# GpSimd's arithmetic in two token mixers handed to VectorE, and modulation rows with places of their own

## The chip, the cores and the metric

The kernel runs on one core of a Trainium2 chip. The core has five engines, each with its own instruction queue, worked in order: TensorE (PE; its weight loads are listed as PEld), VectorE (DVE), ScalarE (ACT), GpSimd (POOL) and SyncE (SP), which issues nearly all DMAs here. Data lie in SBUF (128 partitions) or, behind a matmul, in PSUM banks of 512 columns. The metric is the device time of one execution in microseconds (us).

## The reference, cut to what matters

A backbone of two layers works on 256 latent tokens and 256 context tokens of width 1024. Everything is fp32.

```
for li in range(2):
    sh1, sc1, g1, sh2, sc2, g2 = split(silu(c) @ w_mod[li] + b_mod[li], 6)     # and the same for c_ctx
    h = rms_norm(x) * (1 + sc1) + sh1
    zp, zr, zq, zk, zv, zg = split(h @ w_in[li], ...)
    branches = pool(zp), rwkv7(zr, both directions), attention(zq, zk, zv)     # three mixers
    y = sum_n(sigmoid(zg[n]) * (branches[n] @ w_branch[li, n])) @ w_out[li]
    x = x + g1 * y
    h = rms_norm(x) * (1 + sc2) + sh2
    x = x + g2 * (swiglu(h) if li == 0 else top-2 of 8 experts(h))
```

Context tokens run through layer 0 in full; in layer 1 they only feed the RWKV state and the attention.

## The kernel before

Every large matmul has fp32 accuracy from three passes: a weight tile (128 x 1024, L220, DMA on SP) is split into a rounded part `whi` (ACT, L204) and the rest `wlo` (L208, on DVE or POOL), and whi times x-high, whi times x-low and wlo times x-high are summed in PSUM (L246 to L248, or as a generator L491 to L493). Raw weights, `whi` and `wlo` have two places each in the pool `wa`. In the mixers and in the dense feed-forward every second `wlo` is made by POOL (`lo_mod` 2, `lo_pool` 1), in the experts none.

A mixer has these stages. The front makes the RWKV operands, channel group by channel group and direction by direction (`operands`, L643 to L651), and the pooling; L523 to L527 take each projection out of PSUM with its shift. Then attention, and beside it a triangular solve on DVE (`solve`). Then the core: eight chunks for two directions, each with grams (L871), masks of them on DVE (L882 Ga, L877 Gr), reads (Y, L931), the solved XV (L942 on DVE, L943 on ACT) and the state (XV sum L960, state S L962 on POOL). A chunk of the kept operands comes by DMA (`rakbv`, L845), and its part `Ga` again in a second place (L861), where POOL multiplies it by the decay (L862). Between the core's steps PE is given fill: gate projections and branch merges of the generator `dense`, interleaved by fixed ratios, so PE's order is written out. Readout, merge with the RWKV branch and the output projection follow.

`dense` also advances `mod_slow`: modulation vectors as row products on DVE. A tile of 128 rows of `w_mod2` (128 x 1024) comes by DMA into the next raw weight place (L364), DVE multiplies it by the condition and sums (L368 twice, half a row each, for the context; L370, a whole row in place, for the latents). Layer 0's core does 24 such tiles for layer 0; the dense feed-forward does 56 more.

The scheduler fills DVE, ACT, POOL and SP in the order that its own estimate of times gives; where PE's order is manual it follows the code. Layer 1's second half begins with routing (norm, logits, rank, mask, selection, L1693 to L1794), while the first experts' weights are loaded and split ahead.

```
e = nc.gpsimd if lo_eng == "pool" else nc.vector
e.tensor_tensor(lo, src, hi.bitcast(F32), op=OP.subtract)          # L207, L208
w = self.raw()                                                     # L363, mod_slow
nc.sync.dma_start(a, src[p, :, 64:128])                            # L861, chunk
nc.gpsimd.tensor_tensor(a, a, g[q].to_broadcast([64, 4, 64]), op=OP.mult)
```

Of the kernel before, what the change touches and what calls it, by code (L numbers as in the profile page):

```python
# [19 lines left out]
D = 1024  # L20
# [83 lines left out]
class Builder:  # L104
    def __init__(self, ctx, tc, I, out, dbg=None):
        self.ctx, self.tc, self.nc, self.I, self.out = ctx, tc, tc.nc, I, out
        self.dbg = dbg or {}
        self.nlo, self.lo_first = 0, 0
        self.pre, self.ahead = [], []
        self.raws, self.parted, self.pin = (), (), False  # L110
        self.nraw = self.nparts = 0
        self.banks = {}
        self.norm_banks = ExitStack()
        self.sq = self.rs = None
        self.hw = 512
        self.cpool = ctx.enter_context(tc.tile_pool(name="consts", bufs=1))
        self.dram = ctx.enter_context(tc.tile_pool(name="dr", bufs=1, space=DRAM))
        nc = self.nc
        cst = self.cpool.tile([128, C_N], F32, name="cst")
        nc.sync.dma_start(cst, I["cst"])  # L120
        self.cst = cst
        self.ident = cst[:, C_ID:C_ID + 128]
        self.mask = cst[:, C_MSK:C_MSK + 128]
        self.i2 = cst[:, C_I2:C_I2 + 64]
        self.ob = cst[:, C_OB:C_OB + 128]
        self.ones = cst[:, C_ON:C_ON + 128]
        self.tiny = ctx.enter_context(tc.tile_pool(name="tiny", bufs=6))
        hb = self.cpool.tile([40, 4, 128], F32R, name="hb")
        with tc.tile_pool(name="hb0", bufs=1) as hp:
            hb0 = hp.tile([40, 4, 128], F32, name="hb0")  # L130
            nc.sync.dma_start(hb0, I["heads"])
            nc.vector.tensor_copy(hb, hb0)
        self.hb = hb
        self.vec = []
        for l in range(2):
            v = self.cpool.tile([128, V_N], F32, name=f"vec{l}")
            nc.sync.dma_start(v, I["vec"][l])
            self.vec.append(v)
        self.mod = [[None] * 6 for _ in range(2)]
# [61 lines left out]
    def split(self, hi, lo, src, hi_eng="act", lo_eng="dve"):  # L201
        nc = self.nc
        if hi_eng == "act":
            nc.scalar.copy(hi, src)  # L204
        else:
            nc.vector.tensor_copy(hi, src)
        e = nc.gpsimd if lo_eng == "pool" else nc.vector  # L207
        e.tensor_tensor(lo, src, hi.bitcast(F32), op=OP.subtract)  # L208

    def wload(self, src, n, lo_eng=None, hi_eng="act"):  # L210
# [20 lines left out]
        for s, raw in raws:  # L231
            self.split(hi[:, s], lo[:, s], raw[:, :s.stop - s.start], hi_eng, lo_eng)
        return hi, lo
# [119 lines left out]

    def mod_slow(self, l, j):

        nc = self.nc
        m = self.cpool.tile([128, KD, 2], F32, name=f"mod{l}_{j}")
        b = self.vec[l][:, V_BMOD + 8 * j:V_BMOD + 8 * j + 8]
        ni = 2 if l == 0 or j < 2 else 1
        st = self.mp.tile([128, KD, 2], F32, name="mst", tag="mst")  # L360
        s2 = self.mp.tile([128, KD, 2], F32, name="mst2", tag="mst2")
        for f in range(KD):
            w = self.raw()  # L363
            nc.sync.dma_start(w, self.I["w_mod2"][l, j, f])  # L364
            if ni == 2:
                for h, a in enumerate((st, s2)):
                    k = slice(512 * h, 512 * h + 512)
                    nc.vector.scalar_tensor_tensor(self.scr(), w[:, k], 0.5, self.cb[:, 1, k], op0=OP.mult,  # L368
                                                   op1=OP.mult, accum_out=a[:, f, 1:2])
            nc.vector.scalar_tensor_tensor(w, w, 0.5, self.cb[:, 0], op0=OP.mult, op1=OP.mult,  # L370
                                           accum_out=st[:, f, 0:1])
            yield 3.0
        if ni == 2:
            nc.vector.tensor_tensor(st[:, :, 1], st[:, :, 1], s2[:, :, 1], op=OP.add)
        nc.vector.tensor_tensor(m[:, :, :ni], st[:, :, :ni], b.unsqueeze(2).to_broadcast([128, KD, ni]), op=OP.add)
        self.mod_done(l, j, m[:, :, :ni])
# [174 lines left out]
    def rwkv_front(self, l, full, order):  # L551
# [19 lines left out]
        nc.sync.dma_start(lw, I["lora"][l])  # L571
        self.split(lwh, lwl, lw, "act", "pool")
        self.g2 = sv.tile([96, 512], F32, name="g2")
# [26 lines left out]
        def glo_tile():  # L600
            glo = yield from self.shifted_out(l, 1, T_GLO, full, self.u)
            nc.scalar.activation(glo[0:96, :], glo[0:96, :], AF.Tanh, scale=0.5)
            nc.gpsimd.tensor_scalar(glo[0:96, :], glo[0:96, :], 0.5, 0.5, op0=OP.mult, op1=OP.add)
            self.glo = glo
# [17 lines left out]
        def operands(c, d):  # L622
# [24 lines left out]
                                    n4(G)[:, :, :, :63], o4(kk)[:, :, :, 1:], op=OP.mult)  # L647
            nc.gpsimd.tensor_copy(st[:, :, 1, 0].rearrange("p (s n) -> p s n", s=2), o4(kk)[:, :, :, 0])
            nc.scalar.copy(s4(4), o4(vc))
            nc.gpsimd.tensor_tensor(s4(0), n4(G), o4(rc), op=OP.mult)  # L650
            nc.gpsimd.tensor_tensor(self.order(kd, 0), self.order(kd, 0), self.order(rc, d), op=OP.mult)  # L651
            return st, kd
# [93 lines left out]
    def out_gates(self, l, n, order):  # L746
# [4 lines left out]
        for c in range(4):  # L751
# [5 lines left out]
            gate = self.og.tile([128, n], F32, name="og", tag="og")  # L757
            nc.scalar.copy(gate, gp)
            nc.gpsimd.tensor_scalar(bo, bo, v[:, V_GNB + c:V_GNB + c + 1], None, op0=OP.add)
            nc.gpsimd.tensor_tensor(bo, bo, gate, op=OP.mult)  # L760
            nc.sync.dma_start(self.bonus[c], bo)
            nc.gpsimd.tensor_scalar(gate, gate, v[:, V_GNG + c:V_GNG + c + 1], None, op0=OP.mult)
            nc.sync.dma_start(self.gain[c], gate)
# [75 lines left out]
    def chunk(self, d, n, need_o):  # L839
# [17 lines left out]
        if n:  # L857
            g = self.gq[d][:, :, n - 1].unsqueeze(2)
            for hh, p, q in self.HEADS:
                a = e["Ga"][q, hh]  # L860
                nc.sync.dma_start(a, src[p, :, 64:128])  # L861
                nc.gpsimd.tensor_tensor(a, a, g[q].to_broadcast([64, 4, 64]), op=OP.mult)  # L862
        return e
# [81 lines left out]
    def state(self, e, new, d, n):  # L945
# [15 lines left out]
        for hh, p, q in self.HEADS:  # L961
            nc.gpsimd.tensor_tensor(nS[q], new["XV"][q, hh], g[q].to_broadcast([64, 4, 64]), op=OP.mult)  # L962
        return nS
# [71 lines left out]
    def readout(self, l, n, pool):  # L1035
# [13 lines left out]
        for c in range(4):  # L1049
# [3 lines left out]
            nc.scalar.activation(sq, w, AF.Square)  # L1053
            nc.gpsimd.tensor_tensor(ga[c], ga[c], w, op=OP.mult)
            sqs.append(sq)
# [126 lines left out]
    def pool_branch(self, l, full, order):  # L1182
# [6 lines left out]
        def pool_tile(g):  # L1189
# [10 lines left out]
            for i, z in enumerate(zs):  # L1200
# [3 lines left out]
                while w < win:  # L1204
                    nxt = self.pb.tile([128, 272], F32, name="z", tag="z")
                    nc.gpsimd.tensor_tensor(nxt[:, :m - w], cur[:, :m - w], cur[:, w:m], op=OP.add)
                    cur, m, w = nxt, m - w, 2 * w
                ti = t[:, 256 * i:256 * i + 256]
                nc.gpsimd.tensor_tensor(ti, cur[:, 8 - h:264 - h], iv, op=OP.mult)
                nc.gpsimd.tensor_tensor(ti, ti, z[:, 8:264], op=OP.subtract)  # L1210
            order.add(2, mixed(g, t), self.waits[5] * ns * (g + 4))
# [10 lines left out]

    def branch_split(self, tiles, n, mixed=False):
        res = []
        for t in tiles:
            hi = self.u2(n, F32R)
            lo = self.u2(n, F32R)
            self.split(hi, lo, t, "act", "dve" if mixed and len(res) % 2 == 0 else "pool")
            res.append((hi, lo))
        return res  # L1230

    def merge_branch(self, l, b, br, f, full, gate, acc):
# [8 lines left out]
        if acc is None:  # L1241
            return gate
        nc.gpsimd.tensor_tensor(acc, acc, gate, op=OP.add)
        return acc
# [9 lines left out]
    def merge_steps(self, l, b, br, f, full, gate, acc):  # L1254
# [9 lines left out]
        if acc is not None:  # L1264
            nc.gpsimd.tensor_tensor(acc, acc, gate, op=OP.add)

    def mixer(self, l, x, full, xnew, done=lambda: None):
# [12 lines left out]
        self.sp_small = ex.enter_context(P("small", 1))  # L1280
        self.lo_mod, self.lo_pool, self.lo_first = 2, 1, 2
        self.raws, self.parted = (self.wa, self.wa) + tuple(ex.enter_context(P("w", 1)) for _ in range(l)), (self.wa,)
# [115 lines left out]
        def early_gate(f):  # L1398
            g = lambda n: self.gp.tile([128, n], F32, name="gp", tag="gp")
            self.gate[f] = yield from self.gate_steps(l, 1, f, full, g, "pool")  # L1400

        def dense():
            mods = (t for i in self.parts[4 + l] for t in self.mod_slow(*i))
            br = self.branch_split(self.nat, n)
# [69 lines left out]
        for c in range(4):  # L1474
            self.dump(f"rw{c}", self.wkv[c])
            self.dump(f"nat{c}", self.nat[c])
            self.dump(f"pool{c}", self.pool[c])
        br = self.branch_split(self.wkv, n, True)
        m = []
# [38 lines left out]
    def ffn(self, l, x):  # L1518
        nc, tc, I = self.nc, self.tc, self.I
        with ExitStack() as ex:  # L1520
# [33 lines left out]
            with tc.manual_schedule(engines={mybir.EngineType.PE}):  # L1554
                for f in range(2):
# [10 lines left out]
                    early(f, raws, pss)  # L1566
            mods = (t for i in self.parts[10] for t in self.mod_slow(*i))
            for f in range(2, KF):
# [86 lines left out]
    def moe(self, l, x):  # L1655
        nc, tc, I = self.nc, self.tc, self.I
        ident = self.ident
        with ExitStack() as ex:
# [21 lines left out]
            with P2("scrm2", 3) as self.sp, tc.high_priority(100000):  # L1680
# [40 lines left out]
                keep(nc.vector.tensor_copy(pos, pp.rearrange("p (t e) -> p t e", e=8)))  # L1721
                sel = self.selected(0, pos, msk, two, keep)
                for t in range(2):
# [403 lines left out]
```

## Time and profile before

| | us |
|---|---|
| median of 3 runs | 2495.73 |
| lowest, highest | 2491.53, 2501.99 |
| the profiled execution | 2494.59 |
| its span, first to last instruction | 2492.8 |

Over the span PE is busy 93%, DVE 73%, ACT 51%, POOL 23%, and the DMA queues move 514 MB at a mean of 206 GB/s. By time the stages are, roughly: layer 0's front to 205 us, attention to 410, the core to 655, readout, merge and projection to 780, the dense feed-forward to 1130, layer 1's front to 1300, attention to 1490, the core to 1615, readout and routing to 1690, the experts to the end. Shares over the whole span mix these stages; a stage is read from its own stretch.

[...] A row of waits names who waited and what released it; "issue" means that the profile shows no releaser.

### The profile page before, as it was taken

The numbers are of one execution on the slowest core, as the hardware profiler recorded it, in microseconds if no ns is written. First come the engines' busy times: TensorE is split into PE (matmuls) and PEld (weight loads), VectorE is DVE, ScalarE is ACT, GpSimd is POOL, SyncE is SP. The second block draws the span as 40 slices with busy tenths as digits, with TensorE's granted clock in tenths as the row PEclk, the third lists the DMA queues.
The fourth block names the chain that finished last, engine by engine and source line by source line (L and its number), as shares of the span: only waits on it lengthen the run. The fifth ranks groups of instructions, "written<-read, shape, count | busy, mean of one in ns | idle before, by whom it ended". The sixth has DMA issues, their size and how long they took to land. (4 is left out here: it accounts for less than half of the span.)

```text
span 2492.8 us, 40223 instructions
## 1 busy us (share of the span) xinstructions
PE 2318.3 (93%) x15206; PEld 1858.1 (75%) x15206; DVE 1809.5 (73%) x2723; ACT 1276.6 (51%) x1864; POOL 576.6 (23%) x487
## 2 busy tenths in 40 slices
PE   6899999988899999999779889979999999999998
PEld 4567667777678888777566678768888888888876
DVE  3784667656677656875785755568999999989997
ACT  3553554222243222234554444347777777777775
POOL 1255421243351221122553335430000000000000
PEclk8999998999899999999989989989999999999999
DMA  6364233554433444772473326675999999999995
GB/s 250 95 168 132 77 98 93 173 151 154 144 118 104 150 144 144 235 241 78 128 186 97 116 89 198 194 262 177 367 351 339 360 363 336 343 361 344 356 343 194
DMA packets 224141, 514.33 MB, mean 206 GB/s; under 512 B 70490, under 2 KB 104666, under 8 KB 222786
## 3 DMA queue, kind: packets, MB, share of 16 engines
q1 hardware_dynamic: 223938, 511.67, 61.1%
q8 instruction: 122, 2.00, 0.3%
q14 instruction: 81, 0.66, 0.1%
HBM read 484.79 MB, written 26.74 MB: 205 GB/s over the span
## 5 line engine op out<-in xcount | busy, mean ns | idle before, releaser
L204 ACT CAST whi<-wraw 128x1024 fp32r<-128x1024 f32 (+2 forms) x753 | 754.3, 1019 | 615.9 <-DMA wraw<-in_ffn 178.9
L208 DVE TENSOR_TENSOR wlo<-wraw,whi 128x1024 fp32r<-128x1024 f32 (+2 forms) x629 | 756.4, 1232 | 137.3 <-ACT whi L204 126.5
L208 POOL TENSOR_TENSOR wlo<-wraw,whi 128x1024 fp32r<-128x1024 f32 (+2 forms) x124 | 263.9, 2129 | 722.3 <-ACT whi L204 714.6
L491 PE MATMUL mm<-h,whi 128*128 128x512 f32 (+1 forms) x864 | 347.7, 402 | 33.3 <-DVE s L527 13.6
L493 PE MATMUL mm<-h,wlo 128*128 128x512 f32 (+1 forms) x864 | 321.4, 372 | 11.9 <-DVE wlo L208 6.2
L492 PE MATMUL mm<-h,whi 128*128 128x512 f32 (+1 forms) x864 | 322.0, 373 | 5.5 <-DVE h L476 5.4
L1845 PE MATMUL mm<-whi,xh 128*128 128x512 f32 (+1 forms) x768 | 289.2, 377 | 0.0
L1846 PE MATMUL mm<-whi,xl 128*128 128x512 f32 (+1 forms) x768 | 288.1, 375 | 0.0
L1847 PE MATMUL mm<-wlo,xh 128*128 128x512 f32 (+1 forms) x768 | 281.5, 376 | 1.3 <-DVE wlo L208 1.3
L491 PEld LDWEIGHTS mm<-h,whi 128*128 128x128 f32 x864 | 172.4, 200 | 86.2 <-issue 36.1
L493 PEld LDWEIGHTS mm<-h,wlo 128*128 128x128 f32 x864 | 172.2, 199 | 42.7 <-DVE wlo L208 8.5
L492 PEld LDWEIGHTS mm<-h,whi 128*128 128x128 f32 x864 | 172.9, 200 | 33.5 <-DVE h L476 9.2
L247 PE MATMUL mm<-h,whi 128*128 128x512 f32 (+1 forms) x448 | 170.6, 382 | 2.6 <-DVE h L208 2.6
L248 PE MATMUL mm<-h,wlo 128*128 128x512 f32 (+1 forms) x448 | 170.8, 382 | 0.4 <-POOL wlo L208 0.3
L246 PE MATMUL mm<-h,whi 128*128 128x512 f32 (+1 forms) x448 | 169.8, 380 | 0.0
L1847 PEld LDWEIGHTS mm<-wlo,xh 128*128 128x128 f32 x768 | 144.1, 188 | 29.2 <-DVE wlo L208 2.1
L1846 PEld LDWEIGHTS mm<-whi,xl 128*128 128x128 f32 x768 | 144.4, 188 | 27.0
L1845 PEld LDWEIGHTS mm<-whi,xh 128*128 128x128 f32 x768 | 144.6, 188 | 26.5
L1874 PE MATMUL mm<-wlo,hh 128*128 128x512 f32 x352 | 139.6, 397 | 0.8 <-DVE wlo L208 0.8
L1873 PE MATMUL mm<-whi,hl 128*128 128x512 f32 x352 | 139.1, 395 | 0.0
L1872 PE MATMUL mm<-whi,hh 128*128 128x512 f32 x352 | 138.7, 394 | 0.0
L368 DVE SCALAR_TENSOR_TENSOR scr<-wraw,cb 128x512 f32<-128x512 f32 x96 | 75.7, 806 | 57.6 <-DMA wraw<-in_w_mod 57.0
(378 smaller groups left out, 4024.4 us busy)
## 6 DMA issues: line engine op xcount, KB each, us to landing
wraw<-in_moe SPq DMA_DIRECT2D x516, 512.0 KB, 5.5
wraw<-in_w_in SPq DMA_DIRECT2D x108, 512.0 KB, 3.7
wraw<-in_w_mod SPq DMA_DIRECT2D x96, 512.0 KB, 4.6
wraw<-in_ffn SPq DMA_DIRECT2D x60, 512.0 KB, 3.9
rakbv<-std SPq DMA_DIRECT2D x32, 640.0 KB, 5.3
wraw<-in_w_branch SPq DMA_DIRECT2D x48, 256.0 KB, 2.7
std<-st SPq DMA_DIRECT2D x16, 640.0 KB, 5.0
wraw<-in_w_out SPq DMA_DIRECT2D x13, 512.0 KB, 4.1
```

The costliest lines, as they stand in the source:

```text
L204: nc.scalar.copy(hi, src)
L208: e.tensor_tensor(lo, src, hi.bitcast(F32), op=OP.subtract)
L246: nc.tensor.matmul(ps, wh, xh, start=i == 0, stop=False)
L247: nc.tensor.matmul(ps, wh, xl, start=False, stop=False)
L248: nc.tensor.matmul(ps, wl, xh, start=False, stop=i == n - 1)
L491: nc.tensor.matmul(ps, wh, xh, start=i == 0, stop=False)
L492: nc.tensor.matmul(ps, wh, xl, start=False, stop=False)
L493: nc.tensor.matmul(ps, wl, xh, start=False, stop=i == n - 1)
L1845: nc.tensor.matmul(ps, xh[:, k0 + k], hi[:, w], start=k0 + k == 0, stop=False)
L1846: nc.tensor.matmul(ps, xl[:, k0 + k], hi[:, w], start=False, stop=False)
L1847: nc.tensor.matmul(ps, xh[:, k0 + k], lo[:, w], start=False, stop=k0 + k == 7)
L1874: nc.tensor.matmul(y, hid[k][0], lo[:, w], start=False, stop=k == KF - 1)
```

## The change

In the mixers POOL keeps only its memsets. The weight splits, the splits of activations, the pooling sums, `Ga` and `S` of the core, two operand products, the branch sums and the readout product go to DVE; one small copy, a tanh rescaling and the gate's gain go to ACT; the gate path loses its PSUM copy. The dense feed-forward keeps POOL's splits (`lo_mod` 2 there as before). Layer 0's `mod_slow` no longer takes raw weight places but two half-row tiles from the pool `u` (13 places in layer 0), and its latent product is done in two halves (L374 twice, L377 twice). In the experts the third and the fourth weight split of DVE are ordered behind the last instruction of the selection.

```
-        self.split(lwh, lwl, lw, "act", "pool")
+        self.split(lwh, lwl, lw, "act", "dve")
-            nc.gpsimd.tensor_copy(st[:, :, 1, 0].rearrange("p (s n) -> p s n", s=2), o4(kk)[:, :, :, 0])
+            nc.scalar.copy(st[:, :, 1, 0].rearrange("p (s n) -> p s n", s=2), o4(kk)[:, :, :, 0])
-            nc.gpsimd.tensor_tensor(s4(0), n4(G), o4(rc), op=OP.mult)
-            nc.gpsimd.tensor_tensor(self.order(kd, 0), self.order(kd, 0), self.order(rc, d), op=OP.mult)
+            nc.vector.tensor_tensor(s4(0), n4(G), o4(rc), op=OP.mult)
+            nc.vector.tensor_tensor(self.order(kd, 0), self.order(kd, 0), self.order(rc, d), op=OP.mult)
...
-            nc.scalar.copy(gate, gp)
-            nc.gpsimd.tensor_scalar(bo, bo, v[:, V_GNB + c:V_GNB + c + 1], None, op0=OP.add)
-            nc.gpsimd.tensor_tensor(bo, bo, gate, op=OP.mult)
+            nc.vector.scalar_tensor_tensor(bo, bo, v[:, V_GNB + c:V_GNB + c + 1], gp, op0=OP.add, op1=OP.mult)
...
-                nc.gpsimd.tensor_tensor(a, a, g[q].to_broadcast([64, 4, 64]), op=OP.mult)
+                nc.vector.tensor_tensor(a, a, g[q].to_broadcast([64, 4, 64]), op=OP.mult)
-            nc.gpsimd.tensor_tensor(nS[q], new["XV"][q, hh], g[q].to_broadcast([64, 4, 64]), op=OP.mult)
+            nc.vector.tensor_tensor(nS[q], new["XV"][q, hh], g[q].to_broadcast([64, 4, 64]), op=OP.mult)
...
-        self.lo_mod, self.lo_pool, self.lo_first = 2, 1, 2
+        self.lo_mod, self.lo_pool, self.lo_first = 2, 0, 0
...
-            w = self.raw()
-            nc.sync.dma_start(w, self.I["w_mod2"][l, j, f])
+            ws = place()
+            for s, w in ws:
+                nc.sync.dma_start(w, self.I["w_mod2"][l, j, f][:, s])
...
-            nc.vector.scalar_tensor_tensor(w, w, 0.5, self.cb[:, 0], op0=OP.mult, op1=OP.mult,
-                                           accum_out=st[:, f, 0:1])
+            for (s, w), a in zip(ws, (st, s2)):
+                nc.vector.scalar_tensor_tensor(w, w, 0.5, self.cb[:, 0, s], op0=OP.mult, op1=OP.mult,
+                                               accum_out=a[:, f, 0:1])
...
-            mods = (t for i in self.parts[4 + l] for t in self.mod_slow(*i))
+            mods = (t for i in self.parts[4 + l] for t in self.mod_slow(*i, lambda: [(slice(512 * h, 512 * h + 512), self.u()) for h in range(2)]))
...
+            ins = self.split(hi[:, s], lo[:, s], raw[:, :s.stop - s.start], hi_eng, lo_eng)
+            if self.nlo in self.late_lo:
+                self.behind(ins)
...
-                sel = self.selected(0, pos, msk, two, keep)
+                sel = self.selected(0, pos, msk, two, lambda ins: setattr(self, "mark", keep(ins)))
+
+                self.late_lo = (3, 4)
```

DVE's queue in layer 0's core, one step of the chunks, before: Y copies, a modulation row, the masks.

```order
L931 COPY Y_5056<-ch_5047 128x256
L931 COPY Y_5067<-ch_5058 128x256
L368 SCALAR_TENSOR_TENSOR scr_5390,mst_4882<-wraw_5388,cb_126 128x512
L368 SCALAR_TENSOR_TENSOR scr_5392,mst2_4883<-wraw_5388,cb_126 128x512
L370 SCALAR_TENSOR_TENSOR wraw_5388,mst_4882<-wraw_5388,cb_126 128x1024
L882 TENSOR_TENSOR Ga_5023<-sm_5078,cst_60 64x256
L877 TENSOR_TENSOR Gr_5026<-sm_5078,cst_60 128x256
```

The same engine in a step of layer 0's core now; `u` tiles are modulation rows, L868 is the Ga product that POOL did (L862 before).

```order
L868 TENSOR_TENSOR Ga_4458<-Ga_4458,gq0_3970 64x256 x2
L374 SCALAR_TENSOR_TENSOR scr_4515,mst2_4027<-u_4510,cb_126 128x512
L868 TENSOR_TENSOR Ga_4471<-Ga_4471,gq1_3971 64x256
L377 SCALAR_TENSOR_TENSOR u_4509,mst_4026<-u_4509,cb_126 128x512
L868 TENSOR_TENSOR Ga_4471<-Ga_4471,gq1_3971 64x256
L1271 TENSOR_TENSOR u2_2467<-u2_2467,u_4337 128x512
L888 TENSOR_TENSOR Ga_4458<-sm_4533,cst_60 64x256
L883 TENSOR_TENSOR Gr_4461<-sm_4533,cst_60 128x256
```

The row products still stand ahead of the masks, in more and smaller pieces, and the Ga products, each behind its own DMA, have come in between.

SP's queue in the same core, before: weights and modulation rows take turns in the two raw places.

```order
L845 DMA rakbv_5034<-std01_84 128x4x320
L856 DMA r_5040<-std01_84 64x4x64 x2
L220 DMA wraw_5240<-in_w_in 128x1024
L364 DMA wraw_5388<-in_w_mod2 128x1024
L861 DMA Ga_5023<-std00_83 64x4x64 x2
L861 DMA Ga_5036<-std01_84 64x4x64 x2
L220 DMA wraw_5396<-in_w_in 128x1024
```

SP's queue there now, with half rows into `u`.

```order
L862 DMA r_4758<-std01_84 64x4x64 x2
L867 DMA Ga_4741<-std00_83 64x4x64 x2
L867 DMA Ga_4754<-std01_84 64x4x64 x2
L369 DMA u_4791<-in_w_mod2 128x512
L369 DMA u_4792<-in_w_mod2 128x512
L369 DMA u_4901<-in_w_mod2 128x512
L369 DMA u_4902<-in_w_mod2 128x512
L221 DMA wraw_5193<-in_w_branch 128x512
```

Rows are now asked for two at a time, and no weight load stands behind a row in the same place.

DVE's queue in layer 1's core, where there are no modulation rows, before.

```order
L931 COPY Y_14286<-ch_14277 128x256
L931 COPY Y_14297<-ch_14288 128x256
L1263 SCALAR_TENSOR_TENSOR u_14132<-u_14132,mm_14244 128x256
L882 TENSOR_TENSOR Ga_14253<-sm_14305,cst_60 64x256
L877 TENSOR_TENSOR Gr_14256<-sm_14305,cst_60 128x256
```

And now.

```order
L937 COPY Y_14345<-ch_14336 128x256
L937 COPY Y_14356<-ch_14347 128x256
L1269 SCALAR_TENSOR_TENSOR u_14191<-u_14191,mm_14303 128x256
L868 TENSOR_TENSOR Ga_14312<-Ga_14312,gq0_13412 64x256
L1271 TENSOR_TENSOR u2_12383<-u2_12383,u_14191 128x256
L868 TENSOR_TENSOR Ga_14312<-Ga_14312,gq0_13412 64x256
L209 TENSOR_TENSOR wlo_14515<-wraw_14512,whi_14514 128x1024
L888 TENSOR_TENSOR Ga_14312<-sm_14364,cst_60 64x256
L883 TENSOR_TENSOR Gr_14315<-sm_14364,cst_60 128x256
```

Two Ga products, a branch sum and a weight split, all POOL's or spread over both before, now stand between Y and the masks.

## Rows read from the trace of the kernel before

**Rows 1.** Busy time by stage: stretch, length, engines (instructions), clock, DMA share, GB/s.
```profile
110.00:205.00 95.00, 83.91 (x518) 60.33 (x518) 79.37 (x79) 53.38 (x90) 61.34 (x54) 0.93 0.67 166
...
430.00:655.00 225.00, 201.88 (x2230) 160.18 (x2229) 137.04 (x288) 52.76 (x101) 75.53 (x73) 0.93 0.50 153
...
780.00:1130.00 350.00, 344.47 (x1487) 277.42 (x1486) 236.38 (x349) 100.31 (x138) 75.35 (x33) 1.00 0.55 178
...
1200.00:1300.00 100.00, 80.11 (x624) 63.38 (x623) 82.86 (x91) 60.22 (x104) 57.80 (x51) 0.91 0.66 170
...
1490.00:1615.00 125.00, 119.99 (x1956) 107.18 (x1955) 65.38 (x141) 49.00 (x103) 63.60 (x79) 1.00 0.62 184
...
1690.00:2493.00 803.00, 790.24 (x3829) 655.81 (x3827) 722.96 (x745) 604.48 (x677) 1.82 (x1) 1.00 0.90 327
```

**Rows 2.** PE's waits, 430 to 660: releaser, us in total, times, longest.
```profile
PE sm L871 <- issue: 9.4, 2, 4.8
PE ch L917 <- ACT XV L943: 7.8, 4, 3.9
PE ch L928 <- DVE Ga L882: 3.9, 2, 3.4
PE ch L939 <- DVE Y L931: 1.1, 1, 1.1
PE sm L871 <- DVE Gr L877: 0.7, 3, 0.3
```

**Rows 3.** DVE's groups, 430 to 655: busy us, mean ns, idle before and releaser.
```profile
L368 DVE SCALAR_TENSOR_TENSOR scr<-wraw,cb 128x512 f32<-128x512 f32 x40 | 34.2, 856 | 45.9 <-DMA wraw<-in_w_mod 45.6
...
L882 DVE TENSOR_TENSOR Ga<-sm,cst 64x256 f32<-64x256 f32 x32 | 13.5, 420 | 8.0 <-PE sm L871 7.3
```

**Rows 4.** DVE in order of time, 526 to 546: start, duration, idle before.
```profile
534.87 0.69 DVE L368 SCALAR_TENSOR_TENSOR scr<-wraw,cb 128x512 f32<-128x512 f32 x1 [6.14 <-DMA wraw<-in_w_mod]
...
538.08 0.41 DVE L882 TENSOR_TENSOR Ga<-sm,cst 64x256 f32<-64x256 f32 x1
```

**Rows 5.** PE in order of time, the same stretch.
```profile
538.92 0.76 PE L871 MATMUL sm<-rakbv 64*128 64x128 f32 x2 [4.61 <-issue]
```

**Rows 6.** Waits of the DMA queue SP, 430 to 660.
```profile
SPq L220 <- DVE wraw L370: 42.1, 7, 9.9
SPq L220 <- DVE wlo L208: 19.0, 5, 4.7
```

**Rows 7.** DVE's groups, 1710 to 2490, where POOL is idle.
```profile
L208 DVE TENSOR_TENSOR wlo<-wraw,whi 128x1024 fp32r<-128x1024 f32 x505 | 598.8, 1222 | 46.3 <-ACT whi L204 36.5 <-PE mm L1847 2.9 <-PE sm L1855 2.2
L1860 DVE TENSOR_TENSOR hl<-sm,hh 128x512 fp32r<-128x512 f32 x40 | 27.4, 684 | 0.0
```

**Rows 8.** POOL's groups over the whole span.
```profile
L208 POOL TENSOR_TENSOR wlo<-wraw,whi 128x1024 fp32r<-128x1024 f32 x86 | 210.4, 2448 | 543.6 <-ACT whi L204 536.0 <-DMA wraw<-in_w_in 4.7 <-PE ch L906 2.7
L208 POOL TENSOR_TENSOR wlo<-wraw,whi 128x512 fp32r<-128x512 f32 x34 | 45.9, 1351 | 142.4 <-ACT whi L204 142.3
L962 POOL TENSOR_TENSOR S<-XV,gq 64x256 f32<-64x256 f32 x56 | 40.9, 730 | 62.4 <-DVE XV L960 53.0 <-DVE XV L958 6.2
```

**Rows 9.** DVE's groups in layer 0's front, 110 to 205.
```profile
L643 DVE TENSOR_TENSOR st<-s,s 128x512 f32<-128x512 f32 x8 | 11.9, 1492 | 2.5 <-ACT s L634 2.5
```

**Rows 10.** PE's waits in layer 0's front, 110 to 205.
```profile
PE mm L491 <- DVE s L527: 4.2, 1, 4.2
...
PE mm L493 <- POOL wlo L208: 2.8, 1, 2.8
```

**Rows 11.** PE's waits in layer 1's front and attention, 1200 to 1490.
```profile
PE mm L491 <- DVE s L527: 9.4, 2, 7.9
...
PE sm L1215 <- POOL scr L1210: 2.7, 1, 2.7
```

**Rows 12.** POOL's waits in layer 1's core, 1490 to 1615.
```profile
POOL Ga L862 <- DMA Ga<-std: 29.7, 6, 6.1
```

**Rows 13.** DVE in the routing chain, in order of time.
```profile
1677.77 1.23 DVE L208 TENSOR_TENSOR wlo<-wraw,whi 128x1024 fp32r<-128x1024 f32 x1
```

## What the change will do to the time

> **What bounds the kernel now.** I read the stages first [rows 1]: stage sums with TensorE's (PE's) busy time and granted clock. The experts (1690 to 2493) keep PE busy 790.2 of 803 us at clock 1.00, the dense feed-forward 344.5 of 350: there PE's own work is the time, and no line of the change touches the feed-forward. The room lies in the mixers. In layer 0's core (430 to 655) PE is busy 201.9 of 225 us at a clock of 0.93, in the two fronts 83.9 of 95 and 80.1 of 100 at 0.93 and 0.91; in layer 1's core it is busy 120.0 of 125 at 1.00, so little can be won there, but something can be lost.
>
> Next, who ends PE's waits in layer 0's core [rows 2]: grams 9.4 us, ScalarE's copy of XV 7.8, the mask Ga on VectorE (DVE) 3.9, Y 1.1, Gr 0.7: 22.9 us. All of these lead to one queue. DVE sits idle 45.6 us in that stretch before L368, a modulation row product, until its DMA lands, 40 instructions in 21 tiles [rows 3]. The timeline shows one case whole [rows 4, 5]: DVE waits 6.14 us for a modulation row, works through the three products, reaches the masks of the grams at 538.08, and PE, which needs the masked banks free, stood still 4.61 us until 538.92. The grams themselves had been done long before. Why the row is late stands in the DMA queue's waits [rows 6]: SyncE held weight loads back for 42.1 us until L370 had read a modulation row, since rows and weights share two places.
>
> **The change part by part.**
>
> *Layer 0's modulation rows.* They go from the two weight places to the thirteen u places, each in two halves, and the three products become four. Per row: before 2 of 512 and 1 of 1024 columns, after 4 of 512. Alone these take 684 and 1222 ns [rows 7], so 2590 becomes 2736 ns, plus one more short accumulator read; over 24 rows about 5 us of DVE, beside DVE time that was idle. SyncE issues 24 more DMAs, beside its own waits. What goes is the sharing: a row's DMA no longer waits for a weight split, nor a weight for L370. The 22.9 us of PE's waits are what I can price. I take four fifths of them, 18 us, as the two halves still stand in one in-order DMA queue behind weights and states. The clock: 0.93 over 225 us is 15.8 us lost, and I take it to follow such stops, since the stages without them stand at 1.00; with four fifths of the stops gone I take 12 of it back. Sum 30 us; bounds 38.7 (all of both) and 0 (rows arrive as late as before).
>
> *GpSimd's arithmetic onto DVE.* GpSimd's prices [rows 8] are 2448 ns for a 1024-column weight split, 1351 for one of 512 and 730 for a state product, of whose size the Ga product is too. DVE's own prices for the splits are 1222 and 684 ns [rows 7]; for the two products the nearest row is the mask of the same size, 420 ns [rows 3]. And DVE is slowed while GpSimd works: in layer 0's front the 512-column product L643 takes 1492 ns on average [rows 9] against 684 alone. [...]
>
> Fronts. Freed in layer 0's: 8 times 0.81 = 6.5 us on this line alone, and there are four more of its kind per step, all with two SBUF inputs. Added: 16 products (L650, L651) at 684 ns, 10.9 us, some five splits at 1.22, 6.1, and the pooling adds, some 5. So DVE's load is about what it was; what shrinks is the detour by GpSimd and the single long stalls. PE waited there for L527, queued on DVE, 4.2 and 9.4 us [rows 10, 11], and 2.8 and 2.7 us for GpSimd's own results. Of 19.1 us I take 9, and 3 more of clock: 12. Bounds: 25 gained; 10 lost, if the added products push L527 back instead.
>
> Cores. In layer 0 the 75.5 us of GpSimd [rows 1] become 56 products at 0.42, 7 splits at 1.22, 3 splits and 7 sums at 0.68, 39 us; DVE goes from 137 busy and 46 waiting to about 170 busy of 225. In layer 1 GpSimd's 63.6 us become 56 at 0.42, 4 at 1.22, 7 at 0.68 and 12 at 0.42, 38 us: DVE rises from 65.4 to about 104 of 125, or 83%. The added wait: the Ga product follows a DMA. GpSimd waited 29.7 us for it in layer 1 [rows 12], 14 pairs, some 2 us each; now DVE would wait, with the masks and the XV copy queued behind it, as the order above shows. PE has fill matmuls between a chain step and its user: the 8 chunks share 125 us, 15 to 16 us a chunk with some five steps, so about 3 us a step is my estimate, which covers most of one such wait. I take 8 us for both cores; bounds 0 and 45, the second if all of 29.7 and half as much in layer 0 reach PE.
>
> Small moves: the gate path (L603, L648, L758 to L762) goes to ScalarE and into one DVE instruction per channel; ScalarE is busy 49.0 of 125 and 52.8 of 225 in the cores, which hides it. I price it at nothing; uncovered it is eight activations, under 6 us.
>
> *The two expert splits.* In the routing chain two splits, one of them shown with its 1.23 us [rows 13], stand between the steps of the reciprocal root on which the selection waits. The new order has one left there; the third and fourth stand behind the selection, before the first xl. Gain 1.2 us; bounds 2.4 gained and 1.6 lost, when they delay xl more than they free.
>
> Sum: 30 + 12 - 8 + 1 = 35 us. The profiled execution took 2494.6 us (span 2492.8), 1.1 under the median of 2495.7: 2459.6 there, 2460 as the median.
>
> **The rivals.**
>
> *DVE's queue fills and loses (slower).* Place: layer 1's core and both attention stages. Every chain step (Y, XV, the XV sum) now stands behind splits of 1.22 us and Ga products that wait for DMA. It decides where the Ga data land more than about 3 us after the masks are ready, PE's cover. For it: 83% load and the rows of waiting [rows 12]. Against it: in-order DVE carried 46 us of idle waiting in layer 0 with more work per step, and PE lost 22.9 there. Price: 45 in the cores, 10 in the fronts, against 30 + 1 won by the rows: 24 slower, 2519.
>
> *The modulation rows come as late as before (no change).* The DMA queue is in order: if the halves sit behind weight loads that wait for a split, DVE still waits at L374. For it: 19 us of the DMA queue's waits were for weight splits [rows 6]. Against: the two places now serve weights alone, so each load is asked for one tile sooner. It would give a third of the 30, so 10 + 12 - 8 + 1 = 15: 2480; with the fronts neutral 2492.
>
> *GpSimd's slowing cost more than its waits show (much faster).* Short stalls under half a microsecond, which rows 2 leave out, and low clock in layer 1's front (0.91 of 100 us) and readout go as well: 38.7 + 25 - 3 + 2 = 63: 2432.
>
> **How the numbers follow.** The forecast 2460 (2440 to 2480) 0.57; the late rows 0.20, a quarter of it under 2483; much faster 0.12; slower 0.11. A measurement here can tell about 0.5%, 12.5 us, from no change. Faster by more than that: 0.57 + 0.12 + about 0.05 of the middle one's 0.20 = 0.74; within it 0.16; slower 0.10. The range 2430 to 2498 leaves out the slow rival and the end of the fast one.
>
> **What would show it.** Right: no more than 10 us of DVE's idle time before the row products (L374 in the new numbering) in layer 0; PE's waits at the grams under 5 us; clock in layer 0's core near 0.98; L643 (now L651) near 690 ns in the fronts. Wrong: DVE waiting tens of microseconds for Ga's DMA with PE standing behind the masks (now L888); layer 1's core longer than 125 us; the fronts longer than 95 and 100.

## The result and the profile after

The changed kernel takes 2462.38 us (median of 4 runs, 2459.42 to 2471.82) against 2496.47 for the kernel before (median of 4, 2491.53 to 2501.99): ratio 0.987, 95% interval 0.9848 to 0.9892. 2460 was forecast. The total came out; its largest term did not.

The profiled execution spans 2459.8 us, 33.0 fewer. I cut the span at matmuls that both programs have: a front ends with the last triangle product (`ch<-st`), the attention with the last step of the solve (`ch<-svW,V` or `ch<-V,svW`), a core with its last output (`ch<-Gr,XV`), readout and merge where the next norm's sums begin (`nx<-cst`), the routing where the experts' first `mm<-whi,xh` starts. Lengths in us, "sum" the difference so far:

| stage | before | after | difference | sum |
|---|---|---|---|---|
| start to end of layer 0's front | 211.7 | 199.6 | -12.1 | -12.1 |
| layer 0's attention | 216.9 | 221.1 | +4.2 | -7.9 |
| layer 0's core | 223.1 | 200.1 | -23.0 | -30.9 |
| its readout and merge | 104.2 | 111.3 | +7.1 | -23.8 |
| feed-forward | 388.7 | 389.0 | +0.3 | -23.5 |
| layer 1's front | 169.2 | 164.3 | -4.9 | -28.4 |
| layer 1's attention | 174.2 | 163.4 | -10.8 | -39.2 |
| layer 1's core | 121.2 | 135.0 | +13.8 | -25.4 |
| its readout and merge | 67.0 | 61.2 | -5.8 | -31.2 |
| routing | 14.5 | 12.7 | -1.8 | -33.0 |
| experts to the end | 802.1 | 802.1 | 0.0 | -33.0 |

The stages of after, columns as in [rows 1]; GpSimd (POOL, the fifth pair) is idle in both cores:

```profile
421.00:621.00 200.00, 189.28 (x2205) 150.80 (x2204) 159.10 (x405) 52.80 (x101) 0.00 (x0) 0.97 0.53 165
621.00:732.00 111.00, 98.05 (x396) 73.44 (x396) 78.27 (x149) 40.26 (x65) 4.76 (x2) 0.94 0.37 119
...
1449.00:1584.00 135.00, 123.43 (x1951) 111.46 (x1951) 95.09 (x210) 47.85 (x99) 0.00 (x0) 0.97 0.54 159
...
1658.00:2460.00 802.00, 790.01 (x3828) 655.67 (x3827) 723.44 (x747) 604.74 (x677) 1.81 (x1) 1.00 0.90 328
```

Layer 0's core, PE's waits from 420.7 to 620.8, against [rows 2]: 10.7 us in place of 22.9, and PE's granted clock, the mean share of full speed in the trace, is 0.97 (0.93 before).

```profile
PE sm L877 <- issue: 6.8, 4, 2.8
PE sm L877 <- DVE Gr L883: 2.9, 5, 0.8
PE ch L945 <- DVE Y L937: 1.0, 1, 1.0
```

VectorE's (DVE's) row products there, against [rows 3]: 4.3 us of waiting in place of 45.6, and 684 ns a half in place of 856. The Ga products are new on this engine.

```profile
L374 DVE SCALAR_TENSOR_TENSOR scr<-u,cb 128x512 f32<-128x512 f32 x42 | 28.7, 684 | 4.5 <-DMA u<-in_w_mod 4.3
L377 DVE SCALAR_TENSOR_TENSOR u<-u,cb 128x512 f32<-128x512 f32 x41 | 27.6, 683 | 0.0
...
L868 DVE TENSOR_TENSOR Ga<-Ga,gq 64x256 f32<-64x256 f32 x28 | 11.7, 418 | 4.5 <-DMA Ga<-std 4.2
```

Layer 1's core, where 13.8 us were lost: first PE's waits, then VectorE's group that waits for a DMA.

```profile
PE sm L877 <- issue: 4.6, 4, 1.9
PE sm L877 <- DVE Gr L883: 3.3, 4, 1.0
PE ch L912 <- DVE Ga L888: 1.2, 1, 1.2
```

```profile
L868 DVE TENSOR_TENSOR Ga<-Ga,gq 64x256 f32<-64x256 f32 x28 | 11.7, 418 | 11.8 <-DMA Ga<-std 11.4
```

The readout of layer 0 in order of time: between the head sums and the split that PE waits for stand row products that in before came earlier. PE then waits 7.0 us for ScalarE's `u`, 3.3 in before.

```profile
641.96 0.68 DVE L374 SCALAR_TENSOR_TENSOR scr<-u,cb 128x512 f32<-128x512 f32 x1
...
642.57 0.69 DVE L377 SCALAR_TENSOR_TENSOR u<-u,cb 128x512 f32<-128x512 f32 x1
...
646.78 0.69 DVE L377 SCALAR_TENSOR_TENSOR u<-u,cb 128x512 f32<-128x512 f32 x1
...
647.39 0.69 DVE L374 SCALAR_TENSOR_TENSOR scr<-u,cb 128x512 f32<-128x512 f32 x1
...
648.00 2.49 DVE L1072 TENSOR_TENSOR wk<-wk,ro 128x512 f32<-128x512 f32 x4
```

In layer 0's front L643, now L651, takes 684 ns in place of 1492 [rows 9]:

```profile
L652 DVE SCALAR_TENSOR_TENSOR s<-s,s 128x512 f32<-128x512 f32 x8 | 5.5, 688 | 0.1
...
L651 DVE TENSOR_TENSOR st<-s,s 128x512 f32<-128x512 f32 x8 | 5.5, 684 | 0.0
```

### The profile page after: what moved, and what is told of

Read it like the earlier page. It is cut to its first block, busy times and chain, and to the rows that moved or that the text cites. A ratio compares the mean times of both kernels' runs of the same rounds, so it can differ in the third digit from the quotient of the medians.

```text
span 2459.8 us, 40024 instructions
## 1 busy us (share of the span) xinstructions
PE 2310.2 (94%) x15206; PEld 1851.1 (75%) x15206; DVE 1894.2 (77%) x3133; ACT 1281.2 (52%) x1882; POOL 95.4 (4%) x94
## 5 line engine op out<-in xcount | busy, mean ns | idle before, releaser
L209 DVE TENSOR_TENSOR wlo<-wraw,whi 128x1024 fp32r<-128x1024 f32 (+1 forms) x719 | 838.9, 1193 | 169.8 <-ACT whi L205 158.6
L501 PEld LDWEIGHTS mm<-h,wlo 128*128 128x128 f32 x864 | 171.0, 198 | 37.5 <-DVE wlo L209 11.3
L209 POOL TENSOR_TENSOR wlo<-wraw,whi 128x1024 fp32r<-128x1024 f32 (+1 forms) x34 | 79.4, 2337 | 760.7 <-DMA wraw<-in_ffn 426.6
L251 PEld LDWEIGHTS mm<-h,wlo 128*128 128x128 f32 x448 | 84.5, 189 | 22.3 <-DVE wlo L209 3.3
```

The costliest lines, as they stand in the source:

```text
L209: return e.tensor_tensor(lo, src, hi.bitcast(F32), op=OP.subtract)
L251: nc.tensor.matmul(ps, wl, xh, start=False, stop=i == n - 1)
L501: nc.tensor.matmul(ps, wl, xh, start=False, stop=i == n - 1)
```

## The experiments

Each kernel was timed against the kernel before on its chip; its stages come from one profile. What a profile's stage is worth shows where programs don't differ: over all fourteen, the experts take 800.2 to 804.0 us, the feed-forward 387.2 to 391.1. Below about 4 us one profile tells nothing.

**Each half alone.** `rows_alone` is the kernel before with the new `mod_slow` and its places; `arith_alone` the changed kernel with

```diff
-  self.mod_slow(*i, lambda: [(slice(512 * h, 512 * h + 512), self.u()) for h in range(2)])
+  self.mod_slow(*i, lambda: [(slice(0, D), self.raw())])
```

> The kernel before with one part of the change: layer 0's modulation rows in halves in the u places; GpSimd keeps its arithmetic. Theory (the rows and the weights held each other up in two shared places): layer 0's core falls from 223 to about 200 us, VectorE's idle time before the row products there from 45.6 us to under 10, and the readout behind it loses about 4 of this, so about 2475 us. Rival (GpSimd's slow weight splits held the places, and the rows come late as long as it makes them): less than a third of that, 215 us or more in the core, 2487 us.

> The changed kernel with layer 0's modulation rows back in the two weight places; everything else as changed. Theory (the two parts add up): fronts 17 us shorter, attention 6, routing 2, layer 1's readout 6, layer 1's core 14 longer, layer 0's core within 5 of its 223: about 2480 us, and its gain and that of the rows alone add up to the 33 us of both. Rival (VectorE's added work stands behind the row products' waits): layer 0's core 10 us or more longer than before, 2492 us, and the two gains add up to 10 us less than 33.

| kernel | median us | ratio (95%) | layer 0's core | its readout | both |
|---|---|---|---|---|---|
| rows_alone | 2494.26 | 0.9979 (0.9963 to 0.9995) | 206.0 | 110.3 | 316.3 |
| arith_alone | 2470.40 | 0.9867 (0.9841 to 0.9893) | 206.2 | 106.9 | 313.1 |
| both (after) | 2462.38 | 0.9870 (0.9848 to 0.9892) | 200.1 | 111.3 | 311.4 |

Both expectations missed. The rows alone give 0.2%, 5 us; the arithmetic alone gives as much as the whole change. In layer 0's core each takes 17 us, together 23: two cures for one illness. And the readout behind the core takes 6 of the rows' 17 back. In `rows_alone`, from 430.2 to 636.2, VectorE's wait for rows has fallen to 13.5 us, as the theory had it, but each product is slow beside GpSimd, 980 and 840 ns where after has 684 and 683:

```profile
L371 DVE SCALAR_TENSOR_TENSOR scr<-u,cb 128x512 f32<-128x512 f32 x42 | 41.2, 980 | 13.9 <-DMA u<-in_w_mod 13.5
L374 DVE SCALAR_TENSOR_TENSOR u<-u,cb 128x512 f32<-128x512 f32 x40 | 33.0, 840 | 0.0
```

In `arith_alone` (423.6 to 629.8) rows and weights still share two places, yet the wait has almost halved, from 45.6 to 25.1 us, and SyncE waits 26.8 us for L377 before a weight load where it waited 42.1 for L370 [rows 6]:

```profile
L374 DVE SCALAR_TENSOR_TENSOR scr<-wraw,cb 128x512 f32<-128x512 f32 x39 | 26.8, 687 | 25.5 <-DMA wraw<-in_w_mod 25.1
L377 DVE SCALAR_TENSOR_TENSOR wraw<-wraw,cb 128x1024 f32<-128x1024 f32 x20 | 24.4, 1218 | 0.3
```

**What held the places.** `split0_back` is `arith_alone` with

```diff
+  self.lo_pool = 1 - l      # every second weight split on GpSimd, layer 0's core only
   filled(self.core(full), self.ratio[l])
+  self.lo_pool = 0
```

> As arith_alone (rows in the two weight places), and of layer 0's core nine weight splits (six of 1024 columns, three of 512) go back to GpSimd, the products Ga and S stay on VectorE. Theory (GpSimd's splits of 2.4 us hold the two places that rows and weights share, so that either part of the change cures the same wait): layer 0's core grows from 206 to 217 us or more, VectorE's idle time before the row products from 25 to 40 us or more, about 2482 us. Rival (it was the products Ga and S on GpSimd that slowed VectorE, or stood in GpSimd's queue): 211 us or less, 2474 us.

2488.42 us, ratio 0.9946 (0.9931 to 0.9961); layer 0's core 222.3 us, the length of before. Ten splits on GpSimd (seven of 2.4 us, three of 1.7) put back all 16 us that the arithmetic had won there. VectorE's wait for rows rose to 33.6 us, not to 40, so the wait is part of it; L374 swelled too (815 ns, 687 in `arith_alone`), and SyncE stood 37.5 us for L377 and 10.1 us for GpSimd's splits themselves. In turn VectorE, GpSimd, the DMA queue and PE, 423 to 646:

```profile
L374 DVE SCALAR_TENSOR_TENSOR scr<-wraw,cb 128x512 f32<-128x512 f32 x40 | 32.6, 815 | 34.0 <-DMA wraw<-in_w_mod 33.6
```

```profile
L209 POOL TENSOR_TENSOR wlo<-wraw,whi 128x1024 fp32r<-128x1024 f32 x7 | 16.7, 2392 | 155.5 <-ACT whi L205 137.7 <-PE sm L877 17.8
```

```profile
SPq L221 <- DVE wraw L377: 37.5, 6, 9.8
...
SPq L221 <- POOL wlo L209: 10.1, 3, 5.3
```

```profile
PE sm L877 <- issue: 11.1, 4, 5.0
PE sm L877 <- DMA rakbv<-std: 6.3, 1, 6.3
```

Is it the places, or that GpSimd slows VectorE's own products? With places of their own for the rows, all of GpSimd's arithmetic, slowed products included, costs the core 6 us (206.0 in `rows_alone`, 200.1 in after); with shared places ten splits cost 16. So roughly 10 of the 16 need the sharing; the rest is not told apart. What delayed `rakbv`, a chunk's operands, for which PE waited 6.3 us, was not tried.

**The fronts.** `front_back` is the changed kernel with two products per step on GpSimd again:

```diff
-  nc.vector.tensor_tensor(s4(0), n4(G), o4(rc), op=OP.mult)
-  nc.vector.tensor_tensor(self.order(kd, 0), self.order(kd, 0), self.order(rc, d), op=OP.mult)
+  nc.gpsimd.tensor_tensor(s4(0), n4(G), o4(rc), op=OP.mult)
+  nc.gpsimd.tensor_tensor(self.order(kd, 0), self.order(kd, 0), self.order(rc, d), op=OP.mult)
```

> The changed kernel with the two 512-column products of the fronts (L658 and L659, sixteen each) back on GpSimd. Theory (VectorE's own products swell while GpSimd reads SBUF): L651 to L654 rise from 0.69 to 1 us or more, and of the 17 us that the two fronts won at least 10 are lost, about 2473 us. Rival (weight splits and pooling sums were what counted there): at most 5 lost, 2466 us.

2475.11 us, ratio 0.9891 (0.9874 to 0.9908), beside 0.9881 for `no_late` on the same chip. Layer 0's front ends at 203.4, where the kernels with these products on VectorE end between 198.4 and 201.2: 2 to 5 of 12 us. Layer 1's, 167.7, lies within the others' 163.4 to 169.6. So the rival is nearer for the time, but the slowing is there in layer 0's front (110 to 204): two products of GpSimd a step slow VectorE's L651 and L652, with two SBUF inputs, by some 46% (L653 and L654 by less, to 930 and 769 ns), and L535, which reads PSUM, not at all (739 ns, 743 in after).

```profile
L651 DVE TENSOR_TENSOR st<-s,s 128x512 f32<-128x512 f32 x8 | 8.0, 1003 | 0.0
L652 DVE SCALAR_TENSOR_TENSOR s<-s,s 128x512 f32<-128x512 f32 x8 | 8.0, 1002 | 0.1
...
L535 DVE SCALAR_TENSOR_TENSOR s<-mm,vec,s 128x510 f32<-128x510 f32 x6 | 4.4, 739 | 0.0
```

```profile
L658 POOL TENSOR_TENSOR st<-s,s 128x512 f32<-128x512 f32 x8 | 14.2, 1770 | 43.7 <-ACT s L640 30.4 <-DMA std<-st 7.3 <-issue 6.0
```

The mean hides two kinds. Five of the eight L651 met no product of GpSimd and took 675 to 683 ns; three met one and took 1185, 1721 and 1726 ns, 549 ns more than the time that GpSimd's product ran beside them. Of the six L535 only two met one, and they took 736 and 744 ns. In order of time, each VectorE instruction with GpSimd's beside it, and one that ran alone:

```profile
112.27 1.79 POOL L658 TENSOR_TENSOR st<-s,s 128x512 f32<-128x512 f32 x1 [6.36 <-ACT s L640]
...
112.88 1.73 DVE L651 TENSOR_TENSOR st<-s,s 128x512 f32<-128x512 f32 x1
...
123.05 0.68 DVE L651 TENSOR_TENSOR st<-s,s 128x512 f32<-128x512 f32 x1
...
147.80 0.74 DVE L535 SCALAR_TENSOR_TENSOR s<-mm,vec,s 128x510 f32<-128x510 f32 x1
...
148.01 1.27 POOL L659 TENSOR_TENSOR s<-s,s 128x512 f32<-128x512 f32 x1 [3.67 <-DVE st L651]
```

**The loss in layer 1's core.** `ga_back` and `lo_back` are the changed kernel with, in turn,

```diff
-  nc.vector.tensor_tensor(a, a, g[q].to_broadcast([64, 4, 64]), op=OP.mult)
+  (nc.gpsimd if self.tok0 else nc.vector).tensor_tensor(a, a, g[q].to_broadcast([64, 4, 64]), op=OP.mult)   # layer 1 only
```

```diff
+  self.lo_pool = l          # every second weight split on GpSimd, layer 1's core only
   filled(self.core(full), self.ratio[l])
+  self.lo_pool = 0
```

> The changed kernel with the Ga products of layer 1's core (the 28 that follow a DMA) back on GpSimd. Theory (VectorE waits for these DMAs, with the masks queued behind): layer 1's core falls from 135 to 122 to 126 us, PE's waits at the grams there under 1.5 us, about 2452 us. Rival (it is the length of VectorE's queue, with splits of 1.22 us in front of the masks): at most a third comes back, 130 us or more, 2458 us or more.

> The changed kernel with every second weight split of layer 1's core back on GpSimd, as before the change; the Ga products stay on VectorE. Theory of the DMA waits: at most a third of the 13.8 us comes back, 130 us or more in layer 1's core, 2458 us or more. Rival (queue length): the core falls to 122 to 127 us, about 2452 us.

`ga_back`: 2449.14 us, ratio 0.9788 (0.976 to 0.9816), the core 121.8 us: all of the loss is back. `lo_back`: 2470.34, 0.9885 (0.9857 to 0.9914), the core 137.6: nothing, though ten splits, 9 us of VectorE's work, had left. VectorE's Ga products still wait. It is no clean test of the load, though: what stayed on VectorE swelled beside GpSimd (the Ga products from 418 to 509 ns), and its busy time is 95 us as in after.

```profile
L868 DVE TENSOR_TENSOR Ga<-Ga,gq 64x256 f32<-64x256 f32 x28 | 14.2, 509 | 10.8 <-DMA Ga<-std 10.2
```

In `ga_back` GpSimd does the waiting, and PE's longest group of waits in the core (1450 to 1571.7) is 1.0 us:

```profile
L868 POOL TENSOR_TENSOR Ga<-Ga,gq 64x256 f32<-64x256 f32 x28 | 19.1, 682 | 212.7 <-DVE u L1271 144.6 <-DMA Ga<-std 46.5 <-PE ch L912 11.7
```

```profile
PE sm L877 <- DVE Gr L883: 1.0, 2, 0.5
```

**The wait or the work?** `ga_back` takes both from VectorE. `ga_bufs` was to take the wait alone, `ga_dummy` was to give the work back without it:

```diff
-  for k, bufs in (("Ga", 2), ("XV", 4)):
+  for k, bufs in (("Ga", 4 if self.tok0 else 2), ("XV", 4)):
```

```diff
+  if self.tok0:             # beside ga_back's product on GpSimd
+      z = pl.tile([128, 4, 64], F32, name="dum", tag="dum", bufs=1)
+      nc.vector.tensor_tensor(z[q], self.mask[q, :64].unsqueeze(1).to_broadcast([64, 4, 64]), g[q].to_broadcast([64, 4, 64]), op=OP.mult)
```

> The changed kernel with four buffers for Ga in layer 1's core in place of two, so that SyncE asks for the Ga data before the next rakbv and weight; the products stay on VectorE, their work is the same. Theory (it is the wait for the DMA, not the 11.7 us of products): VectorE's idle time before L868 falls from 11.4 us to under 5, layer 1's core from 135 (139 in no_late) to 123 to 129 us, about 2453 us. Rival (the products themselves, 28 by 0.42 us in VectorE's queue): 132 us or more, 2460 us or more.

> As ga_back, and in layer 1's core 28 products of the same shape and length as the Ga products go onto VectorE beside them; they read two constants, wait for no DMA, and nothing reads their result. Theory (the wait for the DMA is what cost): layer 1's core stays within 4 us of the 121.8 us of ga_back, about 2450 us. Rival (11.7 us more of work in VectorE's queue is enough): 131 us or more, 2458 us or more.

`ga_bufs`: 2463.86 us, 0.9853 (0.9824 to 0.9882), the core 131.5 us. It does not tell them apart: the wait did not fall, as the products moved forward in VectorE's order together with their DMAs: the last starts 28 us before the core's end, 12 in after.

```profile
L868 DVE TENSOR_TENSOR Ga<-Ga,gq 64x256 f32<-64x256 f32 x28 | 11.7, 418 | 12.8 <-DMA Ga<-std 12.3
```

`ga_dummy`: 2448.01 us, 0.9809 (0.9784 to 0.9834), the core 122.8. VectorE carries as much as in after, 96 of 123 us, and the core loses 1.0: VectorE's load over the stage is not what cost.

```profile
1444.30:1567.10 122.80, 119.59 (x1953) 108.36 (x1951) 96.32 (x209) 47.95 (x99) 19.44 (x28) 0.99 0.60 175
```

```profile
L871 DVE TENSOR_TENSOR dum<-cst,gq 64x256 f32<-64x256 f32 x28 | 12.0, 429 | 0.8
```

```profile
L871 DVE TENSOR_TENSOR dum<-cst,gq x28: 407/418/730, 1447.1 to 1473.3; 64x256 f32<-64x256 f32 x28
```

But it does not show that the wait did. All 28 products ran in the first 30 us of the core, where VectorE has idle time (in after it is busy 15.6 us of 30 there); in after the Ga products stand from 1472.8 to 1571.7, among the masks of seven chunks. The steps of after do not follow its waits either. I take a step from one pair of Y copies to the next; in after each of the seven has four Ga products, 1.7 us of work. `ga_dummy` has 13 of its products in step 1, which is 1.3 us longer than in `ga_back`, and none in steps 2 to 7.

| step of layer 1's core | 1 | 2 | 3 | 4 | 5 | 6 | 7 |
|---|---|---|---|---|---|---|---|
| after: waits before L868, us | 1.6 | 2.9 | 0.7 | 0.4 | 2.5 | 2.3 | 1.0 |
| after: length, us | 20.0 | 14.9 | 12.3 | 17.0 | 17.5 | 17.3 | 14.7 |
| `ga_back`: length, us | 18.2 | 13.5 | 11.4 | 14.0 | 15.6 | 15.5 | 12.5 |

The longest wait, 2.9 us, goes with 1.4 us lost against `ga_back`, the shortest, 0.4, with 3.0. In `ga_bufs`, where the last step holds no Ga product any more, that step takes 12.5 us as in `ga_back`. So the products' place on VectorE within the chain costs the 13 us; how much of it is the wait and how much their own 11.7 us there is not shown. The waits of steps 2 and 4 in after:

```profile
1489.66 0.42 DVE L868 TENSOR_TENSOR Ga<-Ga,gq 64x256 f32<-64x256 f32 x1 [2.86 <-DMA Ga<-std]
...
1514.74 0.42 DVE L868 TENSOR_TENSOR Ga<-Ga,gq 64x256 f32<-64x256 f32 x1 [0.42 <-DMA Ga<-std]
```

**The late splits.** `no_late` sets `self.late_lo = ()`.

> The changed kernel without the two late splits of the experts. Theory (two splits of 1.23 us stood between the steps of the root): the stage from the norm to the experts' first matmul grows from 12.7 to 14 to 14.5 us, the whole by 1 to 2, which the time itself can't tell. Rival (the splits only filled idle time of VectorE there): 12.7 us as with them. It also gives the changed kernel, but for this, a second time.

2471.75 us, 0.9881 (0.9863 to 0.9899), which the time does not tell from after. The routing takes 14.5 us, as in before and `rows_alone`; every kernel with the late splits has 12.7 or 12.8.

**Towards a better version.** `ga_rows` is `ga_back` with one more `next(mods, None)` per step; `ga_arith` is `ga_back` with the rows in the weight places; `ga_both` has the Ga products of both layers on GpSimd.

> As ga_back, and layer 0's modulation rows are asked for four at each of the eight steps in place of three, so that all are done before the readout. Theory (half-row products in VectorE's queue made the readout of layer 0 7 us longer): the readout falls from 111 to 104 to 107 us and the core stays within 2 of 200, about 2444 us. Rival (the same products lengthen the core by as much): 2449 us.

> As ga_back, and layer 0's modulation rows are back in the two weight places (arith_alone and ga_back together). Theory (once GpSimd's slow splits are gone, places of their own give the rows nothing that the readout doesn't take back): within 3 us of ga_back, 2449 us, ratio 0.979. Rival (what the profile of arith_alone has longer in layer 0's core, 206 against 200 us, is real): 2455 us, ratio 0.981 to 0.982.

> As ga_back, and layer 0's Ga products go back to GpSimd too. Theory (in layer 0 these waits are hidden, 4.2 us of VectorE's idle time before L868): layer 0's core 198 to 203 us, 2449 us. Rival (VectorE, 159 of 200 us busy, still sets the grams' waits there): 195 us or less, 2443 us. A third outcome (GpSimd's products slow the row products again): L374 and L377 above 0.72 us and 204 us or more.

| kernel | median us | ratio (95%) | layer 0's core | its readout |
|---|---|---|---|---|
| ga_rows | 2447.28 | 0.9782 (0.9767 to 0.9796) | 203.0 | 107.5 |
| ga_arith | 2453.60 | 0.9810 (0.9783 to 0.9837) | 203.4 | 111.8 |
| ga_both | 2440.25 | 0.9759 (0.9731 to 0.9787) | 195.8 | 108.1 |

`ga_rows` moves the rows' work from the readout into the core and wins nothing: the rival. `ga_arith` lies between its two expectations in time and meets the rival's ratio, but its interval overlaps that of `ga_back`. So what places of their own are worth to the rows, once the arithmetic has moved, is 0 and some 5 us by the two pairs of ratios, 2 and 4 us by core and readout together (311.3 in `ga_back`); neither is clear of noise. `ga_both` has the lowest time of all, its interval below that of after, though it overlaps that of `ga_back`. Its core of 195.8 us (198.4 to 203.0 in the other kernels that have the whole change in layer 0) speaks for the rival, and core and readout together, 303.9 us against 310.1 to 314.2 in those kernels, differ by more than one profile's noise: the Ga products count in layer 0 too, where VectorE waited only 4.2 us for them. GpSimd's products cost the row products 21 ns each there (420.7 to 616.5):

```profile
L374 DVE SCALAR_TENSOR_TENSOR scr<-u,cb 128x512 f32<-128x512 f32 x42 | 29.6, 705 | 8.8 <-DMA u<-in_w_mod 8.6
```

## Why the prediction was right, and where not

*What bounds the kernel.* Right: feed-forward and experts did not move, all of the 33 us lies in the mixers and the routing.

*Layer 0's modulation rows, 30 us.* This step failed, inside a right total. Most signs that were named came: waits for rows 4.3 us, clock 0.97. One did not: PE's waits at the grams are 9.7 us, 10.1 before, where under 5 was named; what went are its waits for XV's copy (7.8) and for the mask Ga (3.9). And alone the rows give 5 us, and on top of the arithmetic some 0 to 5, not clear of noise. Two things were wrong. I charged PE's 22.9 us wholly to the sharing of two places; `split0_back` shows that GpSimd's splits of 2.4 us made that sharing dear: the core with shared places takes 222 us with ten of them and 206 without, against 200 with places of their own. The second rival's reading of [rows 6], that weight splits hold the queue, was half of the truth, and I gave it no price on the arithmetic's side. And I priced the core alone: the readout, where the last rows stand before the split that PE waits for, took 6 to 7 us back (4 on top of the arithmetic).

*GpSimd's arithmetic, 12 - 8 us.* Alone it gives 33 us by its ratio (24 between the profiles). The fronts gave 17.0 for 12. The slowing of VectorE was real: in `front_back` the three L651, with two SBUF inputs, that met a product of GpSimd took 1185 to 1726 ns, the five that met none 675 to 683, and two L535, which read PSUM, took 736 and 744 beside one. The masks Ga of layer 0's core, with PSUM as one input, took 420 ns before, with GpSimd busy 75.5 of 225 us [rows 1, 3], and 421 in after, with it idle. But the two products back on GpSimd cost layer 0's front no more than 5 us, so most of its 12 comes from the rest of the move; which part of it was not tried. Not in the sum were the 17 us in layer 0's core, 10.8 in layer 1's attention (160 to 164 us in every kernel with the arithmetic moved, 172 and 174 without) and 5.8 in layer 1's readout, nor the 4.2 lost in layer 0's attention. Of the 10.8, PE's waits for GpSimd's own results in that stage account for 4.5 at most: 2.7, which I had counted to the fronts [rows 11], and 1.8, the row of before below. What brings the rest of these three was not tried.

```profile
PE mm L493 <- POOL wlo L208: 1.8, 1, 1.8
```

*Cores, -8 us.* Mis-sized: layer 1's alone lost 13.8, a sign named for being wrong (longer than 125 us). That was the slower rival's place, and its Ga products were the cause (`ga_back`). My estimate that 3 us a chain step cover a wait failed: VectorE waited 11.4 us, in 8 pieces of 2.9 at most, none over the cover, and the core lost 13. I also spread the 29.7 us of [rows 12] over 14 pairs, 2 us each; the row has six waits, 5 us each on average. And I priced the wait alone and put the products' own 11.7 us in the chain at nothing; what share they have stays open. That a load near 80% is by itself too much, the other half of that rival, was wrong (`ga_dummy`: busy 96 of 123 us, 1.0 us lost).

*The expert splits, 1.2 us:* 1.8, seen in the stage alone.

*The sum.* 35 against 34, by luck in the parts: what I gave to the rows alone in layer 0's core either part brings by itself (17 us each, 23 together), and the 13.8 us lost in layer 1's core were made good by 10.8 and 5.8 in its attention and readout, in kind what the third rival spoke of.

## What to carry to other kernels

Two parts of a change that relieve one queue must not be priced one by one from the same waits: ask of each what the wait would be if the other were already there, and run each alone (here 17 us each in layer 0's core, 23 together). In layer 1's core it was not VectorE's load over the stage that decided, but what stood in its queue between the steps of the chain: 12 us of added work in the first 30 us, where VectorE had idle time, cost 1 us; 28 products among the masks, each behind a DMA, cost 13. So when an engine is cleared of slow arithmetic, try first to leave it the products that wait for a DMA there; here that gave all 13 back. Whether the same products would be free within the chain without their DMA no run shows.

## What was not expected of the hardware

Ten splits on GpSimd, 21.8 us of its time, lengthened a stage of 206 us by 16, though VectorE was busy no longer (156.0 against 157.2 us). Roughly 10 of the 16 came only where rows and weights share places, and SyncE stood 10.1 us there for GpSimd's splits before weight loads; with places of their own for the rows all of GpSimd's arithmetic cost 6. And VectorE's slowing went with its meetings with GpSimd: in `front_back` an L651 that met none took 675 to 683 ns, three that did 549 ns more than the shared time. On the mean that line took 684 ns in after, 1492 beside GpSimd's splits and products in before and 1003 beside two products a step in `front_back`; the row products took 684 in after and 705 beside the small Ga products in `ga_both`.
